# Dilated attention: two streams that keep their tiles and load the next unit over the spent one, in place of three that take new tiles for every unit

## Chip, core and metric

The kernel runs on one core of one Trainium2 chip. The metric is the device time of one execution in microseconds (us). The kernel before takes 1280.46 us (median of 3 runs, 1278.20 to 1281.73).

## What is computed

One decoder layer on x (1024 tokens, width 1024) in float32. Cut to what matters here:

```
h = RMSNorm(x) * (1 + scale(c)) + shift(c);  proj = h @ w_in   # q, k, v, z of A and of B, gates gA, gB
y_a = rms_norm(gated_delta_rule(conv_silu(q_a, k_a, v_a), g, beta)) * silu(z_a) @ w_proj_a
for gi, (win, dil) in enumerate(((128, 1), (512, 4), (2048, 16))):      # 4 heads of 64 each
    o_g, lse_g = dilated_window_attention(q_b, k_b, v_b, win, dil)      # banded blocks of 128
o_b = concat(o_g) * softmax(lse over the three groups)
y_b = (o_b * silu(z_b)) @ w_proj_b
x = x + gate(c) * ((sigmoid(gA) * y_a + sigmoid(gB) * y_b) @ w_out);  out = rms_norm(x) * final_norm_w
```

## The kernel before

Every part of the layer is a generator ("stream"). A planner in the program (`Sched`, line 136) steps the streams one by one while the kernel is built: it keeps a clock per engine with assumed costs, takes the stream of the best priority that is ready by these clocks, and so fixes, once, the order in which instructions stand on each engine. On the chip each engine works through its own list in that order and waits only on semaphores. All large products are split into a rounded high part and a rest, three float32r matmuls each. On the chip all instructions carry line 129, where the recording helper calls the engine, so rows are told apart by tile names.

Names that matter:
- `big`: 34 tiles of 128x1024 in SBUF; `mid`: 6 of 128x512; `wr`: 2, raw weights; `wh`: 6, split weights. `pj` (2 tiles of 128x1024) and `sb` (4 of 128x512) lie in PSUM. `Slots.many(2)` (line 81) takes two tiles at once, `put` gives one back.
- Attention works in 24 units (group g, head pair ti, block pair i2), listed in `todo_a` (line 1649): g = 0 (tile names ..bd 0 and 1), then 1, then 2. `attn_unit` (line 1564) takes two `big` tiles: `buf` for queries, keys and values, `sm2` for the scores. It loads q, k and v from DRAM (`qbd`, `kbd`, `vbd`), computes scores on TensorE (PE) into two `sb` tiles (`sb<-big 64*128`), masks and takes the minimum on VectorE (DVE, `CUSTOM_DVE`), takes Exp on ScalarE (ACT), transposes on PE (`sb<-cst,big`), copies back on ACT, multiplies with the values on PE (`sb<-big,big 128*64`; "PV" below), copies on DVE and stores the result to `ogd`. `buf` is given back after PV, `sm2` after the store is issued. `attn_work` (line 1643) runs this in a loop; `WORKERS` (line 39) such streams run at once, each at its own priority.
- Beside the attention PE works on the last projection products (`pair`, line 710, with `pair_out`, which for the last, z8, takes Silu on ACT in four pieces `mid<-mid` and stores them to `zd`) and, from the last third of the stage, on `tail_products` (line 1884): products pa0 to pa7 with `YA` (loaded from `yad` through `mid`, split on ACT and DVE by `ya_split`, line 1739), then pb0 to pb7 with `YB`, then the output product.
- After the last unit `attn_group` stores the statistics (`std`), `combine` (line 1668) forms the softmax over the groups (`fga`, a transpose `sb<-cst,fga` on PE, `fgd`), and two `yb_split` streams (line 1763) take j = 0 to 5 in turn: per j an `ogd` and a `zd` load, two halves of factors (`mid<-fgd`) multiplied in on DVE, one product with z (permuted for g = 1, 2), and the split into high part (ACT) and rest (DVE). pb0 uses YB[0] to YB[5] in that order, six matmuls each.
- `ya_split` takes tiles only while more than `big.debt + 1` are free, plus `RESERVE` (4) until the attention has ended.
- All DMAs concerned are issued by SyncE (SP) in one list.

Of the kernel before, what the change touches and what calls it, by code (L numbers as in the profile page):

```python
# [15 lines left out]
P = 128  # L16
# [19 lines left out]
BLOCKS = ("B11", "T2", "T1", "B21", "T3", "B22", "T4")  # L36
BLK = "x3"
BLK1 = "T1 T3 T3 T5"
WORKERS = 3
RESERVE = 4  # L40
HPRIO = 8
NW = 8
# [243 lines left out]
def hybrid_block_kernel(ctx: ExitStack, tc: tile.TileContext, x, c, norm_w, ada_w, ada_b, w_tiles, w_vb0, w_vb1,  # L286
                        w_vb2, conv_w, a_log, dt_bias, dn_norm_w, w_pa, w_pb, w_out, final_norm_w, consts, out):
    nc = tc.nc
    S = Sched(nc)
    pe, act, dve, pool, sp = S.pe, S.act, S.dve, S.pool, S.sp  # L290
# [12 lines left out]
    big = Slots(S, bigp, "big", NBIG, [P, T])  # L303
# [40 lines left out]
    vb_d = [dp.tile([T, 256], F32, name=f"vbd{g}") for g in range(3)]  # L344
# [4 lines left out]
    qb_d = [dp.tile([P, T], F32, name=f"qbd{i}") for i in range(6)]  # L349
    kb_d = [dp.tile([P, T], F32, name=f"kbd{i}") for i in range(6)]  # L350
    og_d = [dp.tile([P, T], F32, name=f"ogd{i}") for i in range(6)]
# [446 lines left out]
    ev_hb = {b: [Event() for _ in range(4)] for b in BLOCKS}  # L798
# [96 lines left out]
    ev_qb = [Event() for _ in range(6)]  # L895
    ev_kb = [Event() for _ in range(6)]
# [190 lines left out]
    ev_vbd = [Event() for _ in range(3)]  # L1087
# [473 lines left out]
    ev_og = [Event() for _ in range(3)]  # L1561
    pend = [0, 0, 0]

    def attn_unit(g, i2, ti):

        i0 = 2 * i2
        kf = max(i0 - 1, 0) if g == 0 else i0
        n_ = i0 + 2 - kf
        buf, sm2 = yield from big.many(2)
        qt, kt = buf[:, 0:256], buf[:, 256:256 + n_ * P]  # L1570
        v3 = buf[:, 640:640 + n_ * P].rearrange("p (a f) -> p a f", f=P)
        sp.dma_start(qt, qb_d[2 * g + ti][:, i0 * P:(i0 + 2) * P])
        sp.dma_start(kt, kb_d[2 * g + ti][:, kf * P:(i0 + 2) * P])
        if g == 0:
            src = vb_d[g].rearrange("(i p) f -> p i f", p=P)[:, kf:kf + n_]
        elif g == 1:
            src = vb_d[g].rearrange("(b p r) f -> r p b f", b=2, r=4)[i2]
        else:
            src = vb_d[g].rearrange("(p r) f -> p r f", r=8)[:, i0:i0 + 2]
        sp.dma_start(v3, src[:, :, ti * P:(ti + 1) * P])  # L1580
        yield
        tiles = []
        for i in (i0, i0 + 1):
            prev = (g == 0 and i > 0) or (g == 1 and i % 2 == 1)
            tiles.append((i, i % 2, (i - 1 if prev else i) - kf, 256 if prev else 128))
        sms = [sm2[:, sl] for sl in HALVES]
        pbs = yield from sb.many(2)
        for i, a, k0, nk in tiles:
            for hd in range(2):
                r = slice(64 * hd, 64 * hd + 64)  # L1590
                pe.matmul(pbs[hd][:, a * 256:a * 256 + nk], qt[r, a * P:(a + 1) * P], kt[r, k0 * P:k0 * P + nk], start=True,
                          stop=True)
        yield
        for hd in range(2):
            h4 = 2 * ti + hd
            sm = sms[hd]
            for i, a, k0, nk in tiles:
                msk = amask2 if g == 2 else amask if nk == 256 else amask[:, P:2 * P]
                dve.tensor_tensor_reduce(sm[:, a * 256:a * 256 + nk], pbs[hd][:, a * 256:a * 256 + nk], msk, -0.125, 3e38,
                                         op0=OP.add, op1=OP.min, accum_out=st_a[g][:, i, h4, 0:1])  # L1600
            sb.put()
            yield
            for i, a, k0, nk in tiles:
                s_ = sm[:, a * 256:a * 256 + nk]
                act.activation(s_, s_, AF.Exp, bias=st_a[g][:, i, h4, 0:1], scale=-1.0,
                               accum_out=st_a[g][:, i, h4, 1:2])
        yield
        pts = []
        for hd in range(2):
            pb = yield from sb.get()  # L1610
            n = 0
            for i, a, k0, nk in tiles:
                for b in range(nk // P):
                    pe.transpose(pb[:, n * P:(n + 1) * P], sms[hd][:, a * 256 + b * P:a * 256 + (b + 1) * P], ident)
                    n += 1
            yield
            pt = sms[hd]
            act.activation(pt[:, 0:n * P], pb[:, 0:n * P], AF.Copy)
            sb.put()
            pts.append(pt)  # L1620
        yield
        pb = yield from sb.get()
        n = 0
        for i, a, k0, nk in tiles:
            nb = nk // P
            for b in range(nb):
                for hd in range(2):
                    vv = v3[:, k0 + b, hd * 64:hd * 64 + 64]
                    pe.matmul(pb[64 * hd:64 * hd + 64, a * P:(a + 1) * P], vv, pts[hd][:, n * P:(n + 1) * P],
                              start=b == 0, stop=b == nb - 1)  # L1630
                n += 1
        yield
        big.put()
        dve.tensor_copy(pts[0][:, 0:2 * P], pb[:, 0:2 * P])
        sb.put()
        yield
        sp.dma_start(og_d[2 * g + ti][:, 2 * i2 * P:2 * (i2 + 1) * P], pts[0][:, 0:2 * P])
        big.put()
        pend[g] += 1
        if pend[g] == 8:  # L1640
            S.set(ev_og[g])

    def attn_work():
        while todo_a:
            g, ti, i = todo_a.pop(0)
            yield [ev_vbd[g], ev_qb[2 * g + ti], ev_kb[2 * g + ti], *ev_hb["T4"]]
            yield from attn_unit(g, i, ti)

    todo_a = [(g, ti, i) for g in range(3) for ti in range(2) for i in range(4)]

# [352 lines left out]
    for g in range(3):  # L2003
        S.add(combine(g), 7.5, f"combine{g}")
    for q in range(WORKERS):
        S.add(attn_work(), 6 + 0.1 * q, f"attnw{q}")
# [74 lines left out]
```

## Time and profile before

| | |
|---|---|
| median of 3 runs | 1280.46 us |
| the profiled execution | 1279.4 us, its span 1277.7 us |
| PE matmul busy | 1252.2 us of the span, 98% |
| DVE, ACT busy | 766.9 us, 497.9 us |
| granted PE clock, mean | 0.995 of 2.4 GHz |
| attention units on PE | from 867.6 to 1045.9 us |

The profile is one execution. A row of the timeline gives start, duration, engine, operation, output tile <- input tiles, shape, the number of merged instructions, and in brackets how long the engine sat idle before and what ended that. Matmuls are pipelined, so a merged group's duration holds the tail of its last one; start to start is the better price. "DMA to landing" counts from the issue to the arrival of the data.

### The profile page before, as it was taken

To read this page: it belongs to the slowest core of one execution; us is meant where nothing else is said; L and a number is where in the kernel's file an instruction comes from. 1 tells how busy PE (TensorE), PEld (TensorE's weight loads), DVE (VectorE), ACT (ScalarE), POOL (GpSimd) and SP (SyncE) were. 2 spreads that over 40 slices of the span, in tenths; PEclk is the share of its full clock that TensorE was granted. 3 is DMA by queue.
4 is the path that set the end of the run, shared out by engine and by line. 5 is a ranking of instruction groups with operands and counts; after the bars stand their busy time and mean duration, and the time that the engine had idled before them with its cause. 6 is when DMAs were issued, how large, how long until landed. Compare 5 with 4: busy or idle time off the path is not lost.

```text
span 1277.7 us, 19213 instructions
## 1 busy us (share of the span) xinstructions
PE 1252.2 (98%) x7302; PEld 1030.8 (81%) x7302; DVE 766.9 (60%) x1528; ACT 497.9 (39%) x1079; POOL 173.9 (14%) x128
## 2 busy tenths in 40 slices
PE   7999999999999999999999999999999999999997
PEld 3689888988888978888888888887777678878886
DVE  5845893457874367864579834555555546655533
ACT  5525622346223345233462335325555852122211
POOL 4700300033001022000320002300000000002400
PEclk9999999999999999999999999999999999999999
DMA  9534433143322262341343222645455758843422
GB/s 356 200 109 148 120 92 88 67 155 114 112 75 75 73 209 65 102 115 69 107 127 103 83 76 78 225 149 156 145 137 149 251 178 255 231 162 113 143 94 83
DMA packets 112558, 172.03 MB, mean 135 GB/s; under 512 B 41009, under 2 KB 72913, under 8 KB 112466
## 3 DMA queue, kind: packets, MB, share of 16 engines
q1 hardware_dynamic: 112322, 170.55, 42.4%
q8 instruction: 57, 0.93, 0.3%
q14 instruction: 35, 0.29, 0.1%
q10 hardware_dynamic: 144, 0.26, 0.1%
HBM read 123.40 MB, written 47.37 MB: 134 GB/s over the span
## 4 chain that ended last, share of the span: by engine, by line
PE 88%; DVE 3%; DMA 3%; ACT 2%; issue 2%; POOL 1%; SPq 0%; POOLq 0%; ACTq 0%; DVEq 0%
PE pj L129 67%; PE sb L129 22%; DVE big L129 2%; ACT big L129 1%; DMA wr<-in_w_out_dram 1%; DMA big<-kbd 1%; POOL big L129 1%; DMA big<-gd 0%; ACT wh L129 0%; DVE mid L129 0%; DVE wh L129 0%; DMA wr<-in_w_pa_dram 0%; POOL wh L129 0%; ACT L129 0%; SPq L129 0%
## 5 line engine op out<-in xcount | busy, mean ns | idle before, releaser
L129 PE MATMUL pj<-big,wh 128*128 128x512 f32 x3356 | 825.2, 398 | 0.8 <-DVE big L129 0.5
L129 PEld LDWEIGHTS pj<-big,wh 128*128 128x128 f32 x3356 | 617.2, 189 | 131.9 <-issue 9.9
L129 ACT ACTIVATE wh<-wr 128x1024 fp32r<-128x1024 f32 (+3 forms) x99 | 97.5, 985 | 239.7 <-PE pj L129 223.1
L129 DVE TENSOR_TENSOR wh<-wr,wh 128x1024 fp32r<-128x1024 f32 (+3 forms) x96 | 115.2, 1200 | 64.2 <-ACT wh L129 64.0
L129 ACT ACTIVATE big<-big 128x1024 f32<-128x1024 f32 (+2 forms) x77 | 74.1, 969 | 187.2 <-DVE big L129 133.3
L129 PE MATMUL pj<-wh,big 128*128 128x256 f32 (+2 forms) x702 | 110.6, 308 | 0.5 <-POOL wh L129 0.3
L129 PE MATMUL sb<-big,wh 128*128 128x512 f32 x368 | 105.1, 423 | 0.0
L129 PEld LDWEIGHTS pj<-wh,big 128*128 128x128 f32 x702 | 96.2, 189 | 6.2 <-POOL wh L129 0.7
L129 DVE SCALAR_TENSOR_TENSOR big<-pj,cw,big 128x1023 f32<-128x1023 f32 (+2 forms) x72 | 92.1, 1279 | 1.7
L129 PEld LDWEIGHTS sb<-big,wh 128*128 128x128 f32 x368 | 66.9, 190 | 21.1 <-issue 8.4
L129 DVE TENSOR_TENSOR big<-big,big 128x1024 f32<-128x1024 f32 (+4 forms) x44 | 57.8, 1316 | 25.9 <-ACT big L129 18.8
L129 PE MATMUL sb<-sq,big 128*128 128x128 f32 x464 | 67.9, 278 | 3.0 <-ACT sq L129 2.2
L129 PEld LDWEIGHTS sb<-sq,big 128*128 128x128 f32 x464 | 63.4, 193 | 8.8 <-ACT sq L129 3.1
L129 POOL TENSOR_TENSOR wh<-wr,wh 128x1024 fp32r<-128x1024 f32 x3 | 9.1, 3036 | 348.8 <-ACT wh L129 348.8
L129 ACT ACTIVATE big<-sb 128x512 f32<-128x512 f32 (+2 forms) x80 | 40.9, 522 | 39.6 <-PE sb L129 39.5
L129 DVE SCALAR_TENSOR_TENSOR sq<-sq,gsm,sb 128x128 f32<-128x128 f32 x48 | 16.6, 345 | 63.4 <-PE sb L129 62.2
L129 DVE CUSTOM_DVE_ANT_0 big<-sb,cst 128x128 f32<-128x128 f32 (+1 forms) x96 | 29.0, 348 | 39.7 <-PE sb L129 39.7
L129 PEld LDWEIGHTS sb<-cst,big 128*128 128x128 f32 x268 | 33.9, 145 | 22.7 <-DVE rstd L129 6.8
L129 PE MATMUL sb<-cst,big 128*128 128x128 f32 x268 | 43.5, 284 | 8.0 <-DVE rstd L129 4.9
L129 PE MATMUL pj<-big,big 128*128 128x512 f32 x210 | 49.2, 390 | 0.0
L129 ACT ACTIVATE mid<-sb 128x512 f32<-128x512 f32 (+3 forms) x48 | 24.0, 500 | 60.9 <-PE sb L129 60.5
L129 DVE TENSOR_TENSOR mid<-big 64x31 f32<-64x31 f32 (+15 forms) x124 | 41.2, 332 | 8.4 <-POOL big L129 4.9
(140 smaller groups left out, 1283.5 us busy)
## 6 DMA issues: line engine op xcount, KB each, us to landing
wr<-in_w_tiles_dram SPq DMA_DIRECT2D x64, 512.0 KB, 4.2
big<-in_ada_w_dram SPq DMA_DIRECT2D x24, 512.0 KB, 9.0
big<-in_x_dram SPq DMA_DIRECT2D x16, 512.0 KB, 5.2
gd<-big SPq DMA_DIRECT2D x16, 512.0 KB, 2.9
big<-gd SPq DMA_DIRECT2D x16, 512.0 KB, 5.2
big<-grow SPq DMA_DIRECT2D x8, 512.0 KB, 5.7
vtd<-big SPq DMA_DIRECT2D x8, 512.0 KB, 2.6
big<-vtd SPq DMA_DIRECT2D x32, 128.0 KB, 4.5
```

The source lines that it names most:

```text
L129: r = f(*a, **k)
```

## The change

A stream now takes its two tiles once. While a unit is under way it already takes the next one from `todo_a`: behind the first head's masking on DVE, with the scores computed, it issues the next unit's k and q loads over the spent ones in the same `buf`, and behind PV the next v load. The scores of a unit wait for its own k and q event, PV for its own v event. The output copy goes to another place, since `buf` and `sm2` stay in use. k is loaded ahead of q. There are two such streams, not three, so four `big` tiles are held in place of six.

```diff
-WORKERS = 3
+WORKERS = 2
-    def attn_unit(g, i2, ti):
...
-        buf, sm2 = yield from big.many(2)
-        qt, kt = buf[:, 0:256], buf[:, 256:256 + n_ * P]
-        v3 = buf[:, 640:640 + n_ * P].rearrange("p (a f) -> p a f", f=P)
-        sp.dma_start(qt, qb_d[2 * g + ti][:, i0 * P:(i0 + 2) * P])
-        sp.dma_start(kt, kb_d[2 * g + ti][:, kf * P:(i0 + 2) * P])
...
+    def attn_needs(u):
+        g, ti, i2 = u
+        return [ev_vbd[g], ev_qb[2 * g + ti], ev_kb[2 * g + ti], *ev_hb["T4"]]
+    def attn_ahead(u, buf, what, ev):
+        last, done = S.cur.last, dict(S.cur.done)
+        attn_load(u, buf, what)
+        S.set(ev)
+        S.cur.last, S.cur.done = last, done
+    def attn_unit(u, buf, sm2, evs):
...
+        yield evs[:1]
         pbs = yield from sb.many(2)
...
+            if hd == 0 and todo_a and all(e.t is not None for e in attn_needs(todo_a[0])):
+                nxt = todo_a.pop(0)
+                ahead = [Event(), Event()]
+                attn_ahead(nxt, buf, "k", ahead[0])
...
         yield
+        yield evs[1:]
         pb = yield from sb.get()
...
-        big.put()
-        dve.tensor_copy(pts[0][:, 0:2 * P], pb[:, 0:2 * P])
+        o_ = pts[0][:, 0:2 * P]
+        if nxt is None:
+            big.put()
+        else:
+            attn_ahead(nxt, buf, "v", ahead[1])
+            o_ = pts[1][:, 0:2 * P] if g == 0 else buf[:, 512:768]
+        dve.tensor_copy(o_, pb[:, 0:2 * P])
...
+        return (nxt, ahead) if nxt else (None, None)
     def attn_work():
         while todo_a:
...
+            buf, sm2 = yield from big.many(2)
...
+            while u is not None:
+                u, evs = yield from attn_unit(u, buf, sm2, evs)
```

The planner then orders everything behind the first unit anew. Three places:

On SP, in the last third of the attention (`kbd_185`, `qbd_179`, `vbd_119` are keys, queries and values of group 2's second head pair, `yad` loads feed `ya_split`, `gd` loads are gates). Before:

```order
L129 DMA big_9047<-gd_129 128x1024
L129 DMA ogd_190<-big_8856 128x256
L129 DMA big_9057<-qbd_179 128x256
L129 DMA big_9057<-kbd_185 128x256
L129 DMA big_9057<-vbd_119 128x2x128
L129 DMA mid_9073<-yad_125 128x512
```

With the change:

```order
L129 DMA big_8997<-gd_129 128x1024
L129 DMA big_7588<-kbd_185 128x256
L129 DMA big_7588<-qbd_179 128x256
L129 DMA big_8659<-vbd_119 128x2x128
L129 DMA ogd_190<-big_8659 128x256
L129 DMA mid_9036<-yad_125 128x512
```

Keys and queries of one stream's next unit now stand apart from values, and the values that stand next are the other stream's.

On ACT, where the Silu pieces of z8 (`mid<-mid`) meet the Exp of the attention (`big,sta<-big,sta`); copies of transposes are `big<-sb`, high parts of YA `big<-mid`, weight splits `wh<-wr`. Before:

```order
L129 ACT_TABLE_LOAD
L129 ACTIVATE mid_8899<-mid_8899 128x512
L129 ACTIVATE big_8766<-sb_8875 128x256
L129 ACTIVATE wh_8891<-wr_8805 128x1024
L129 ACTIVATE mid_8869<-mid_8869 128x512
L129 ACTIVATE wh_8959<-wr_8908 128x1024
L129 ACTIVATE mid_8782<-mid_8782 128x512
L129 ACT_TABLE_LOAD
L129 ACTIVATE big_8856,sta_105<-big_8856,sta_105 128x128 x2
```

With the change, from behind the third Silu piece on:

```order
L129 ACT_TABLE_LOAD
L129 ACTIVATE big_8660,sta_105<-big_8660,sta_105 128x128 x2
L129 ACTIVATE big_7589<-sb_8909 128x256
L129 ACTIVATE big_8839<-mid_8841 128x512
L129 ACTIVATE big_8839<-mid_8876 128x512
L129 ACTIVATE wh_8932<-wr_8905 128x1024
L129 ACT_TABLE_LOAD
L129 ACTIVATE mid_8772<-mid_8772 128x512
L129 ACTIVATE big_8660<-sb_8949 128x256
L129 ACTIVATE big_8660<-sb_8955 128x256
L129 ACT_TABLE_LOAD
L129 ACTIVATE big_7589,sta_105<-big_7589,sta_105 128x128 x2
```

An Exp now stands between the third and the fourth Silu piece, so this stretch has two table loads more.

On DVE, from the output of pa7 (the first row of each; `pj_9742` before, `pj_9693` now) to that of pb0 (the last). `big<-mid,big` is half a product with the factors, `128x8x128` the permuted product with z, the row of 128x768 a weight split. Before:

```order
L129 SCALAR_TENSOR_TENSOR big_9740<-big_9740,pj_9742 128x1024
L129 TENSOR_TENSOR big_9769<-mid_9781,big_9769 128x512
L129 TENSOR_TENSOR wh_9822<-wr_9686,wh_9821 128x768
L129 TENSOR_TENSOR big_9769<-mid_9828,big_9769 128x512
L129 TENSOR_TENSOR big_9778<-big_9778,big_9769 128x8x128
L129 TENSOR_TENSOR big_9865<-big_9778,big_9864 128x1024
L129 SCALAR_TENSOR_TENSOR big_9818<-big_9818,pj_9820 128x1024
```

With the change:

```order
L129 SCALAR_TENSOR_TENSOR big_9691<-big_9691,pj_9693 128x1024
L129 TENSOR_TENSOR wh_9776<-wr_9642,wh_9775 128x768
L129 TENSOR_TENSOR big_9735<-mid_9739,big_9735 128x512
L129 TENSOR_TENSOR big_9703<-mid_9757,big_9703 128x512
L129 TENSOR_TENSOR big_9706<-big_9706,big_9703 128x8x128
L129 TENSOR_TENSOR big_9735<-mid_9791,big_9735 128x512
L129 TENSOR_TENSOR big_9736<-big_9736,big_9735 128x8x128
L129 TENSOR_TENSOR big_9813<-big_9706,big_9812 128x1024
L129 TENSOR_TENSOR big_9819<-big_9736,big_9818 128x1024
L129 SCALAR_TENSOR_TENSOR big_9772<-big_9772,pj_9774 128x1024
```

Before, only YB[5] (`big_9865`) was finished between the two outputs and YB[4] ahead of them. Now the second half of YB[4] (`big_9813`) and YB[5] (`big_9819`) both stand there.

## Rows read from the trace of the kernel before

**Rows 1.** The page's busy times (us, share of the span, instructions).

```profile
PE 1252.2 (98%) x7302; PEld 1030.8 (81%) x7302; DVE 766.9 (60%) x1528; ACT 497.9 (39%) x1079; POOL 173.9 (14%) x128
```

**Rows 2.** The view of waits of PE over the whole span: who ended the idle time, us in total, times, the longest.

```profile
PE sb L129 <- DMA big<-kbd: 2.5, 4, 1.8
...
PE sb L129 <- ACT big L129: 1.3, 2, 1.0
```

**Rows 3.** The timeline of PE from 1012 to 1042 us.

```profile
1016.17 0.71 PE L129 MATMUL sb<-cst,big 128*128 128x128 f32 x2 [1.04 <-ACT big L129]
...
1018.22 0.66 PE L129 MATMUL sb<-big,big 128*64 128x128 f32 x8
1018.81 0.44 PE L129 MATMUL sb<-cst,big 128*128 128x128 f32 x2
1019.00 0.71 PE L129 MATMUL pj<-big,wh 128*128 128x512 f32 x2
...
1021.05 0.71 PE L129 MATMUL sb<-big 64*128 64x128 f32 x8 [0.20 <-DMA big<-kbd]
1021.70 0.66 PE L129 MATMUL sb<-big,big 128*64 128x128 f32 x8
1022.29 3.06 PE L129 MATMUL pj<-big,wh 128*128 128x512 f32 x12
...
1028.73 1.13 PE L129 MATMUL sb<-big 64*128 64x128 f32 x8 [1.76 <-DMA big<-kbd]
1029.79 4.17 PE L129 MATMUL pj<-big,wh 128*128 128x512 f32 x12
```

**Rows 4.** Stretches of 2 us: busy time of PE, weight loads, DVE, ACT and POOL, each with its number of instructions, then the granted clock, the DMA share and GB/s.

```profile
1028.00:1030.00 2.00, 1.27 (x9) 1.08 (x10) 0.17 (x1) 0.33 (x1) 0.00 (x0) 0.72 0.70 227
1030.00:1032.00 2.00, 2.00 (x5) 1.60 (x6) 1.97 (x10) 1.95 (x8) 0.00 (x0) 0.50 0.95 277
1032.00:1034.00 2.00, 2.00 (x10) 1.34 (x9) 0.00 (x0) 1.60 (x6) 0.00 (x0) 0.93 0.92 299
```

**Rows 5.** Stretches of 2 us at 452 us, the same columns.

```profile
452.00:454.00 2.00, 1.63 (x7) 1.35 (x6) 0.90 (x4) 0.68 (x3) 0.00 (x0) 0.50 1.09 380
454.00:456.00 2.00, 2.00 (x10) 1.76 (x9) 0.87 (x5) 0.59 (x3) 1.29 (x1) 0.64 0.99 293
```

**Rows 6.** The timeline of PE at 451 us.

```profile
451.39 0.49 PE L129 MATMUL sb<-sq,big 128*128 128x128 f32 x2 [1.80 <-ACT sq L129]
```

**Rows 7.** The chain of waits from 1018 to 1030 us: start, us, what.

```profile
1021.69 6.90 DMA big<-kbd
```

**Rows 8.** The DMA issues by form: KB each, median us from issue to landing.

```profile
mid<-fgd SPq DMA_DIRECT2D x24, 128.0 KB, 6.5
...
big<-kbd SPq DMA_DIRECT2D x18, 128.0 KB, 3.1
```

**Rows 9.** The view of waits of all engines from 865 to 1050 us, columns as in the waits of PE.

```profile
ACT big L129 <- DMA mid<-yad: 4.2, 4, 3.4
```

**Rows 10.** The timeline of ACT from 975 to 1002 us.

```profile
976.23 1.06 ACT L129 ACTIVATE wh<-Xb 128x1024 fp32r<-128x1024 f32 x1
...
992.42 0.63 ACT L129 ACTIVATE mid<-mid 128x512 f32<-128x512 f32 x1
993.07 1.28 ACT L129 ACT_TABLE_LOAD   x1
994.36 0.40 ACT L129 ACTIVATE big<-big,sta 128x128 f32<-128x128 f32 x1
...
995.52 0.58 ACT L129 ACTIVATE mid<-sb 128x512 f32<-128x512 f32 x1
...
1000.75 1.14 ACT L129 ACTIVATE big<-mid 128x512 fp32r<-128x512 f32 x2
1001.79 0.36 ACT L129 ACTIVATE big<-sb 128x256 f32<-128x256 f32 x1
```

**Rows 11.** The timeline of DVE from 1100 to 1126 us.

```profile
1109.56 2.17 DVE L129 TENSOR_TENSOR big<-big,big 128x1024 f32<-128x1024 f32 x1
1112.91 1.23 DVE L129 TENSOR_TENSOR big<-big,big 128x1024 fp32r<-128x1024 f32 x1 [1.18 <-ACT big L129]
1115.97 1.22 DVE L129 SCALAR_TENSOR_TENSOR big<-big,pj 128x1024 f32<-128x1024 f32 x1 [1.84 <-DMA big<-gd]
1117.11 0.69 DVE L129 TENSOR_TENSOR big<-mid,big 128x512 f32<-128x512 f32 x1
1117.71 0.95 DVE L129 TENSOR_TENSOR wh<-wr,wh 128x768 fp32r<-128x768 f32 x1
1118.70 0.69 DVE L129 TENSOR_TENSOR big<-mid,big 128x512 f32<-128x512 f32 x1
1119.43 2.18 DVE L129 TENSOR_TENSOR big<-big,big 128x1024 f32<-128x1024 f32 x1
1122.73 1.23 DVE L129 TENSOR_TENSOR big<-big,big 128x1024 fp32r<-128x1024 f32 x1 [1.13 <-ACT big L129]
```

**Rows 12.** The timeline of ACT from 1108 to 1126 us.

```profile
1121.64 1.06 ACT L129 ACTIVATE big<-big 128x1024 fp32r<-128x1024 f32 x1 [5.27 <-DVE big L129]
```

**Rows 13.** The timeline of PE from 1068 to 1126 us.

```profile
1070.33 53.16 PE L129 MATMUL pj<-big,wh 128*128 128x512 f32 x232
1124.02 2.34 PE L129 MATMUL pj<-big,wh 128*128 128x512 f32 x9 [0.53 <-DVE big L129]
```

More of the change, by code (lines that the diff above doesn't have):

```diff
@@ L1562, in hybrid_block_kernel, with attn_place @@
     pend = [0, 0, 0]
-    def attn_unit(g, i2, ti):
+    def attn_place(u, buf):
+        g, ti, i2 = u
         i0 = 2 * i2
@@ L1568, in attn_unit, with attn_load @@
         n_ = i0 + 2 - kf
-        buf, sm2 = yield from big.many(2)
-        qt, kt = buf[:, 0:256], buf[:, 256:256 + n_ * P]
-        v3 = buf[:, 640:640 + n_ * P].rearrange("p (a f) -> p a f", f=P)
-        sp.dma_start(qt, qb_d[2 * g + ti][:, i0 * P:(i0 + 2) * P])
-        sp.dma_start(kt, kb_d[2 * g + ti][:, kf * P:(i0 + 2) * P])
[L1574 to L1581, printed above, removed]
+        v = 640 if g == 0 else 768
+        return (buf[:, 0:256], buf[:, 256:256 + n_ * P],
+                buf[:, v:v + n_ * P].rearrange("p (a f) -> p a f", f=P), i0, kf, n_)
+    def attn_load(u, buf, what):
+        g, ti, i2 = u
+        qt, kt, v3, i0, kf, n_ = attn_place(u, buf)
+        if "k" in what:
+            sp.dma_start(kt, kb_d[2 * g + ti][:, kf * P:(i0 + 2) * P])
+            sp.dma_start(qt, qb_d[2 * g + ti][:, i0 * P:(i0 + 2) * P])
+        if "v" in what:
+            if g == 0:
+                src = vb_d[g].rearrange("(i p) f -> p i f", p=P)[:, kf:kf + n_]
+            elif g == 1:
+                src = vb_d[g].rearrange("(b p r) f -> r p b f", b=2, r=4)[i2]
+            else:
+                src = vb_d[g].rearrange("(p r) f -> p r f", r=8)[:, i0:i0 + 2]
+            sp.dma_start(v3, src[:, :, ti * P:(ti + 1) * P])
+    def attn_needs(u):
+        g, ti, i2 = u
+        return [ev_vbd[g], ev_qb[2 * g + ti], ev_kb[2 * g + ti], *ev_hb["T4"]]
[5 more added lines that the diff above has]
+    def attn_unit(u, buf, sm2, evs):
+        g, ti, i2 = u
+        qt, kt, v3, i0, kf, n_ = attn_place(u, buf)
         tiles = []
@@ L1593, in attn_unit @@
         yield
+        nxt = None
         for hd in range(2):
@@ L1632, in attn_unit @@
         yield
-        big.put()
-        dve.tensor_copy(pts[0][:, 0:2 * P], pb[:, 0:2 * P])
+        o_ = pts[0][:, 0:2 * P]
+        if nxt is None:
+            big.put()
+        else:
+            attn_ahead(nxt, buf, "v", ahead[1])
+            o_ = pts[1][:, 0:2 * P] if g == 0 else buf[:, 512:768]
+        dve.tensor_copy(o_, pb[:, 0:2 * P])
         sb.put()
         yield
-        sp.dma_start(og_d[2 * g + ti][:, 2 * i2 * P:2 * (i2 + 1) * P], pts[0][:, 0:2 * P])
-        big.put()
+        sp.dma_start(og_d[2 * g + ti][:, 2 * i2 * P:2 * (i2 + 1) * P], o_)
+        if nxt is None:
+            big.put()
         pend[g] += 1
@@ L1641, in attn_unit @@
             S.set(ev_og[g])
+        return (nxt, ahead) if nxt else (None, None)
     def attn_work():
         while todo_a:
-            g, ti, i = todo_a.pop(0)
-            yield [ev_vbd[g], ev_qb[2 * g + ti], ev_kb[2 * g + ti], *ev_hb["T4"]]
-            yield from attn_unit(g, i, ti)
+            u = todo_a.pop(0)
+            yield attn_needs(u)
+            buf, sm2 = yield from big.many(2)
+            evs = [Event(), Event()]
+            attn_load(u, buf, "k")
+            S.set(evs[0])
+            attn_load(u, buf, "v")
+            S.set(evs[1])
+            while u is not None:
+                u, evs = yield from attn_unit(u, buf, sm2, evs)
     todo_a = [(g, ti, i) for g in range(3) for ti in range(2) for i in range(4)]
```

## The prediction

> **What bounds the kernel now.** I read the page's busy times first: matmuls cover 1252.2 us of the span of 1277.7 us [rows 1]. So an edit is worth what it takes from or adds to PE's idle time, or to the time in which PE runs at its lower clock; what ACT, DVE or the DMAs gain elsewhere is worth nothing. Next the waits of PE: the attention's scores wait four times for keys, 2.5 us in all, the longest 1.8 us, and its transposes and PV twice for ACT, 1.3 us [rows 2]. That is 3.8 us, and the timeline shows where nearly all of it lies: between 1014 and 1029 us, the last third of the attention [rows 3]. The reader should see there that the scores at 1028.73 us waited 1.76 us for keys, and that the twelve matmuls behind them took 4.17 us where the same twelve at 1022.29 us took 3.06. The granted clock explains it: 0.72, 0.50 and 0.93 in three stretches of 2 us [rows 4], so PE stood at its 1.2 GHz level for most of it, and 0.56 + 1.00 + 0.14 = 1.7 us were lost. The same happened behind a wait of 1.80 us at 451 us [rows 6], with 0.50 and 0.64, again 1.7 us [rows 5]. The wait of 1.04 us [rows 3] cost no clock. The attention thus costs at most 3.8 + 1.7 = 5.5 us that a change of its loads could give back, 0.43%.
>
> **Keys and queries ahead.** The keys behind the long wait took 6.90 us from issue to arrival [rows 7]; the median is 3.1 us [rows 8]. Now a unit's keys and queries are issued right behind the previous scores of the same stream. Between a score block of the last third and the next one of its stream PE has, by the new order, some 22 matmuls of 512 columns (0.229 us each, 53.16/232, [rows 13]), three pairs of transposes, two PVs and one block of scores. Start to start these are 0.19, 0.59 and 0.65 us [rows 3]: 5.0 + 0.6 + 1.2 + 0.7 = 7.5 us, above even the 6.90. So I take the waits for keys, 2.5 us, as gone, and the fall of the clock behind them, 1.7 us. What is late next is ACT.
>
> **Two more table loads on ACT.** Before, three Silu pieces of z8 share one load; now an Exp stands between the third and the fourth, and the stretch has four loads in place of two. A load takes 1.28 us, and the Exp starts 0.01 us behind it [rows 10]. In the new order, from the copy of z8's T1 product to the second Exp pair of the unit two further on, ACT has that copy (0.58), 8 Exps (3.2), 4 loads (5.1), 3 Silus (1.9), 2 weight splits (2.1), 4 copies (1.4) and 6 halves of YA (3.4): 17.8 us, durations from [rows 10]. In the same piece of order PE has 52 matmuls (11.9), five pairs of transposes (1.0), two PVs (1.2) and two score blocks (1.3): 15.3 us. Both work through their lists in order and PE needs those Exps, so it stands for 2.5 us, in pieces of at most about 1.2 us; without the two loads the lists would be even. The halves of YA also hang on their loads, which now stand behind a weight load that waits for a split. ACT waited for them 4.2 us before, at most 3.4 at once [rows 9]; the new lateness lies between 0 and 3.4 us, and I take 0.8, nearer to the shorter ones, since half a unit's work lies ready on PE there. Together 3.3 us of new idle time.
>
> ScalarE: Activation LUTs in the Trainium skill, section What ACT_TABLE_LOAD costs, puts a switch at 1283 ns for the load and 1380 ns more for a drain, 2.66 us, which speaks against this change more strongly. The trace agrees on the load and shows no drain [rows 10]. By the page two more switches would cost 5.3 us on ACT, an estimate, and the time would come to 1285.9 us; by the rows it stays with 2.56 us on ACT.
>
> The attention as a whole: 3.3 - 5.5 = **-2.2 us**. Its bounds: -5.5 if every wait goes; if YA is late by the full 3.4 us and the clock falls once, 2.5 + 3.4 + 1.7 - 5.5 = +2.1.
>
> **The end of the attention's chain: YB.** pb0 is the first product that needs YB, 32 matmuls in for the rest of YB[5]. Before, that is the one wait behind the attention: PE ran 232 matmuls from 1070.33 to 1123.49 us and then stood 0.53 us until DVE had finished YB[5] at 1123.96 [rows 11, 13]. Counted back, pb0 began at 1116.0 and DVE began on pa7's output at 1115.97, at the same moment. From there DVE needed 8.0 us: output, factor half, weight split, factor half, permuted product, a pause of 1.1 us for ACT's high part [rows 12], rest.
>
> In the new order DVE has from pa7's output to the rest of YB[5]: output (1.14 start to start), weight split (0.97), two factor halves (0.6 and 0.73), permuted product (2.17), factor half (0.73), permuted product (2.18), and two rests (1.2 each) [rows 11]. That is 10.9 us, and 9.7 us to the rest of YB[4]; the pause for ACT is filled by the first of the two rests. DVE cannot start on any of it before pa7 has ended, since the output stands first in its list. pb0 needs the rest of YB[4] after 26 matmuls, 5.95 us, so PE stands 1.2 us for YB[4]'s high part and then about 2.4 us for its rest. Matmul 32 runs at about 11.1 us behind pa7's end, where it ran at 8.05 before: **+3.1 us**. A wait of 2.4 us is longer than both after which the clock fell [rows 3, 6], so I add the 1.7 us that each of those cost: **+4.8 us**. Bounds: 0.5 us less than 3.1 if DVE's starts pack closer, and 4.8. Behind pb0 PE is the bound up to the end, so nothing gives this back.
>
> **At nothing.** The 72 loads of the attention and its 24 stores are the same in number and size; queries and keys change places. Values are issued behind PV and needed at the next PV, one whole unit later; as before, SP stands for PV's end there, and behind it in its list wait the other stream's store and the YA loads, whose lateness is counted above. The statistics' store slips behind a weight load, but the transposes of the factors move back on PE by 16, 6 and 6 matmuls too, and YB is needed only at pb0. Two `big` tiles more are free; PE waits for no tile now. The factors of YB[5] take 6.5 us to land [rows 8] and are issued more than 9 us ahead, under pa7.
>
> **Sum.** -2.2 + 4.8 = +2.6 us. The profiled execution took 1279.4 us, so such a one would take 1282.0. It lies 1.1 us below the median of 1280.46, which I take as the base: **1283.1 us**. About 0.3%, 3.8 us, is what a measurement of this kernel can tell from no change; the forecast lies inside it.
>
> **Rivals.**
> - *The waits for keys go and the tail is hidden* (faster): -4.2 us from the keys alone, 1276.3 us. For it: the loads do move ahead by more than their landing time. Against it: DVE's list at pb0 is fixed by the order, with PE idle there already [rows 13]. 0.10.
> - *Level*: the attention loses all its 5.5 us and the wait at pb0 brings no fall of the clock: -2.4 us; with half of the attention's gain, +0.4. About 1279.5 us. 0.16.
> - *ACT becomes the bound of the last third* (slower): the two streams leave PE less other attention work while ACT switches tables, one wait grows past 1.8 us and the clock falls there too: 2.1 + 4.8 = +6.9 us, 1287.4 us. It decides from 1.8 us in one piece on. For it: 17.8 us on ACT against 15.3 on PE. Against: the waits come in pieces with matmuls between. 0.20.
> - *The loads don't come earlier*, because SP stands at a value load for PV or for a store: the 2.5 + 1.7 us stay, and the 2.5 of ACT are added to the 1.3 there was: about +1.7 in the attention and 4.8 at the tail, 1287.0 us. 0.06.
>
> **Chances.** The forecast's own case 0.48, from +0.5 to +5 us; something over a quarter of it lies beyond 3.8 us. Slower by over 0.3%: 0.13 + 0.20 + 0.06 = 0.39. Faster by over 0.3%: 0.09, most of the first rival. Within: 0.52. The range reaches from the first rival's time to the two slow ones: 1276.5 to 1287.5 us; the forecast's own is 1281.0 to 1285.5.
>
> **What would show it.** Right: the row of waits for `big<-kbd` is empty or under 0.5 us; PE waits for DVE `big` in pb0 some 3.6 us in two pieces, with a granted clock near 0.5 in a stretch behind; PE waits for ACT 2 to 4 us between the z8 product and the end of the attention, with four table loads there. Wrong: if pb0 starts without a wait, the tail's step fails and the time falls to 1276 to 1279 us; if keys are still waited for, the first step fails; if PE waits for ACT no more than before, the table loads were hidden.

## Result and profile after

| | before | after |
|---|---|---|
| median | 1278.46 us (22 runs, 1276.41 to 1283.93 and one of 7092.59) | 1284.83 us (22 runs, 1281.02 to 1289.79) |
| ratio after to before | | 1.0043, 95% interval 1.0032 to 1.0053 |
| profiled execution, span | 1279.4, 1277.7 us | 1281.23, 1279.5 us |
| granted clock, mean | 0.995 | 0.996 |

Slower by 0.43%, 5.5 us; the ratio is taken without the one slow run of the kernel before, and the two medians alone stand 6.4 us apart. The two profiled executions differ by 1.8 us only: that of before lies 0.9 us above its median, that of after 3.6 us below. So the page of after was a lucky one, and the medians have to be explained from more than one trace (first experiment). The waits of PE after, from 860 to 1130 us, which answer to [rows 2]:

```profile
PE pj L129 <- DVE big L129: 2.3, 1, 2.3
PE pj L129 <- ACT big L129: 1.8, 2, 1.4
PE sb L129 <- DMA big<-qbd: 0.4, 1, 0.4
```

The waits for keys are gone; 0.4 us for queries is left, at the first unit of all. PE's wait for ACT in the attention is one of 0.35 us, for a high part of YA, though ACT now loads its table four times there. In these timelines of PE and of ACT the wait ends 1.5 us behind the last of the four:

```profile
1020.48 1.03 PE L129 MATMUL pj<-big,wh 128*128 128x512 f32 x2 [0.35 <-ACT big L129]
```

```profile
1007.12 1.28 ACT L129 ACT_TABLE_LOAD   x1
...
1010.79 1.28 ACT L129 ACT_TABLE_LOAD   x1
...
1015.24 1.28 ACT L129 ACT_TABLE_LOAD   x1
...
1017.73 1.28 ACT L129 ACT_TABLE_LOAD   x1
1019.03 0.40 ACT L129 ACTIVATE big<-big,sta 128x128 f32<-128x128 f32 x1
```

The tail is what the forecast said. The timeline of PE, which answers to [rows 13]: two waits in pb0, 3.7 us, where there was one of 0.53.

```profile
1104.75 13.31 PE L129 MATMUL pj<-big,wh 128*128 128x512 f32 x58
1119.48 0.73 PE L129 MATMUL pj<-big,wh 128*128 128x512 f32 x2 [1.42 <-ACT big L129]
1122.52 27.74 PE L129 MATMUL pj<-big,wh 128*128 128x512 f32 x114 [2.31 <-DVE big L129]
```

The clock behind them, in stretches of 2 us (columns as in [rows 4]): it stands at its 1.2 GHz level for most of 1123 to 1127 us, which costs 0.88 + 0.82 = 1.7 us.

```profile
1123.00:1125.00 2.00, 2.00 (x7) 1.55 (x6) 0.68 (x1) 0.00 (x0) 0.00 (x0) 0.56 0.00 0
1125.00:1127.00 2.00, 2.00 (x7) 1.53 (x6) 0.39 (x1) 0.84 (x1) 0.00 (x0) 0.59 0.00 0
1127.00:1129.00 2.00, 2.00 (x10) 1.66 (x9) 1.97 (x2) 0.00 (x0) 0.00 (x0) 1.00 0.00 0
```

DVE, as in [rows 11]: nothing from 1108.2 until pa7 ends at 1112.66, and then the nine instructions, up to 1123.7 us.

```profile
1107.55 0.69 DVE L129 TENSOR_TENSOR big<-mid,big 128x512 f32<-128x512 f32 x1 [1.16 <-DMA mid<-fgd]
1112.66 1.22 DVE L129 SCALAR_TENSOR_TENSOR big<-big,pj 128x1024 f32<-128x1024 f32 x1 [4.42 <-PE pj L129]
1113.80 0.95 DVE L129 TENSOR_TENSOR wh<-wr,wh 128x768 fp32r<-128x768 f32 x1
1114.66 1.49 DVE L129 TENSOR_TENSOR big<-mid,big 128x512 f32<-128x512 f32 x2
1116.19 2.15 DVE L129 TENSOR_TENSOR big<-big,big 128x1024 f32<-128x1024 f32 x1
1118.52 0.69 DVE L129 TENSOR_TENSOR big<-mid,big 128x512 f32<-128x512 f32 x1 [0.19 <-DMA mid<-fgd]
1119.25 4.43 DVE L129 TENSOR_TENSOR big<-big,big 128x1024 f32<-128x1024 f32 x3
```

### The profile page after: what moved, and what is told of

The parts are those of the page before. It is cut to its first block, busy times and chain, and to the rows that moved or that the text cites. A ratio compares the mean times of both kernels' runs of the same rounds, so it can differ in the third digit from the quotient of the medians.

```text
span 1279.5 us, 19222 instructions
## 1 busy us (share of the span) xinstructions
PE 1252.6 (98%) x7302; PEld 1029.3 (80%) x7302; DVE 766.2 (60%) x1528; ACT 502.2 (39%) x1081; POOL 173.6 (14%) x128
## 4 chain that ended last, share of the span: by engine, by line
PE 80%; DMA 5%; DVE 5%; issue 4%; ACT 3%; POOL 2%; SPq 0%; POOLq 0%; DVEq 0%; ACTq 0%
PE pj L129 60%; PE sb L129 20%; DVE big L129 3%; DMA big<-in_x_dram 2%; ACT big L129 1%; DMA wr<-in_w_out_dram 1%; DMA big<-grow 1%; POOL big L129 1%; POOL wh L129 1%; DVE wh L129 1%; ACT L129 1%; DVE mid L129 1%; ACT wh L129 0%; DMA mid<-yad 0%; SPq L129 0%
## 5 line engine op out<-in xcount | busy, mean ns | idle before, releaser
L129 ACT ACTIVATE big<-big,sta 128x128 f32<-128x128 f32 (+1 forms) x96 | 42.2, 442 | 13.0 <-DVE sta L129 12.9
```

The lines of the kernel that those rows point to most:

```text
L129: r = f(*a, **k)
```

## The experiments

In the table each trace is cut at the first score F: front (up to F - 1 us; the same order of instructions in all these kernels, up to the attention's first loads), attention (from there to F + 182), pb0 (F + 243 to F + 275). Idle is a stretch less the time in which PE was busy; clock is the length times one minus the granted clock, both added up over pieces of 2 us. "Busy" is the time from F to the first matmul of pb0 less the idle and clock in it. Each ratio below is to the kernel before on the same chip.

| trace | front idle, clock | attention idle, clock | pb0 idle, clock | busy |
|---|---|---|---|---|
| before, page | 13.6, 3.4 | 3.83, 1.70 | 0.55, 0 | 242.6 |
| before, again | 14.6, 1.7 | 3.03, 0 | 0.85, 0 | 242.7 |
| after, page | 14.5, 1.7 | 1.19, 0 | 3.73, 1.70 | 244.7 |
| after, again | 13.9, 3.4 | 1.42, 0 | 4.60, 1.70 | 244.7 |
| after, third | 16.0, 6.9 | 2.31, 0 | 4.23, 3.40 | 245.1 |
| output moved | 16.3, 6.8 | 2.37, 0 | 2.57, 1.70 | 245.1 |
| output, split moved | 14.2, 0 | 1.18, 0 | 5.09, 3.40 | 244.2 |
| before, both moved | 16.0, 3.4 | 3.42, 1.70 | 1.70, 0 | 242.5 |
| three streams | 13.9, 3.4 | 7.13, 0 | 1.94, 0 | 244.9 |
| before, two streams | 13.6, 3.4 | 3.27, 3.42 | 16.06, 8.92 | |
| early statistics | 15.7, 5.1 | 2.32, 0 | 0.54, 0 | 245.1 |
| the same, both moved | 16.9, 6.9 | 1.29, 0 | 1.06, 0 | 244.2 |
| before, early statistics | 13.7, 3.4 | 2.91, 0 | 0.64, 0 | 242.8 |
| early statistics, Silu held | 14.1, 0 | 3.79, 0 | 2.14, 1.70 | 244.3 |

### Both kernels again

No edit.

> The kernel before, unchanged: a second profiled execution of it. Theory A: the 1.76 us wait for keys at 1028 us and the fall of the clock behind it (1.7 us) belong to the first profiled execution and not to most, so here the waits of the scores for keys are under 1.5 us in sum, the granted clock stays at 1.0 between 1014 and 1040 us and the execution takes about 1279.4 - 3 = 1276.4 us, the lowest of its 22 runs. Rival B: the same wait for keys of 1.5 to 2.0 us with the clock near 0.5 behind it, and about 1279 us.

> The changed kernel, unchanged: a second profiled execution, since the first (1281.2 us) stands 3.6 us below the median of 1284.8. Theory A: PE waits at pb0 as in the first, 1.4 us for ACT and 2.3 us for DVE, and what makes most executions longer than the first is the clock: a mean of 0.991 to 0.994 in place of 0.996, with a second fall somewhere; I expect it to be longer at pb0 (the clock at 0.5 for 6 us in place of 3.5). Rival B: the second fall lies in the attention, behind a wait of PE for ACT of over 1.5 us between 1010 and 1030 us, where four table loads stand.

> The changed kernel again, timed on the same chip as the others of this group and for a third trace: ratio to the kernel before 1.003 to 1.005; PE stands 3.5 to 4.7 us at pb0 in two pieces, the clock falls behind them (1.8 us lost), and waits for 1.2 us or less in the attention.

Before: 1276.81 us, span 1275.1. After: 1284.92 us once, and 1286.06 us (12 runs; 1.0049, 1.0033 to 1.0066). Theory A holds for the kernel before: the wait at 1028 us was 1.04 us there, and no fall of the clock followed, as the timeline and the stretches of that execution show.

```profile
1027.63 0.72 PE L129 MATMUL sb<-big 64*128 64x128 f32 x8 [1.04 <-DMA big<-kbd]
```

```profile
1026.00:1028.00 2.00, 0.96 (x13) 0.75 (x14) 0.42 (x1) 0.00 (x0) 0.00 (x0) 1.00 1.04 372
1028.00:1030.00 2.00, 2.00 (x14) 1.57 (x12) 1.66 (x10) 1.41 (x3) 0.00 (x0) 1.00 0.92 275
```

So of the 5.5 us that the forecast counted as recoverable, 1.7 belong to some executions only (two of the four traces of kernels with the old attention), and 0.8 of idle time likewise. After: the clock fell behind pb0's waits in all three traces, once for twice as long, which A had expected of the second; nothing fell in the attention, so rival B is out. What also shows is the front: 14.1 to 23.7 us are lost there over all traces, in the same order of instructions, with up to 6.9 us of it by the clock. With a spread of 9.6 us in the front alone, one page says little about 0.4%.

### What pb0 waits for: DVE's order

```diff
     def pa_out(pt, t, j):
+        if j == 7:
+            yield ev_ybs[5]
         dve.scalar_tensor_tensor(t, t, 1.0, pt, op0=OP.add, op1=OP.mult)
...
-            yield u.raw_ev
+            yield [u.raw_ev, ev_ybs[5]] if u is pb_units[2] else u.raw_ev
```

The first hunk alone is the run "output moved"; both are "output, split moved", and in the kernel before "before, both moved".

> The changed kernel with one DVE instruction moved: pa7's output product (1.14 us) stands behind the rests of YB[4] and YB[5] in DVE's list in place of ahead of them, so DVE can work on both while pa7 still runs. Theory A: the whole of PE's wait at pb0 goes, 1.4 + 2.3 us, and the fall of the clock behind it, 1.7 us: 5.4 us less than the changed kernel, 1279.4 us in the median, ratio to the kernel before 1.000 to 1.002. Rival B (most of the loss against before lies in the attention): less than 2.5 us is won, 1282.5 us or more, ratio over 1.0025.

> The changed kernel with both DVE instructions that hang on pa7's end put behind the rests of YB[4] and YB[5]: pa7's output product and the weight split of pb2 (its ACT half and its loads move with it). Moving the output alone took 1.1 us off the wait at pb0, since the weight split behind it waits for tiles that pa7 frees. Theory A: now nothing ahead of YB's work waits for pa7's end; PE's wait at pb0 falls from 3.7 to 4.6 us to under 0.8, the clock does not fall behind it, and the time is 5.5 us under that of the changed kernel on the same chip: ratio to the kernel before 0.998 to 1.000. Rival D (the loss lies elsewhere, in the 866 us of the same order): the wait goes and the ratio stays over 1.002. Rival E (YB's high parts wait for tiles of YA that pa7 frees): over 2 us of the wait stay.

> The kernel before with the same two instructions moved behind YB[5]'s rest. There PE waited only 0.5 to 0.9 us at pb0: those go, ratio to the kernel before 0.9993 to 0.9997, below what the runs can tell. If instead the ratio is over 1.002, then moving the weight split and the output costs something itself (pb1's start, pb2's weights), and the run before last must be read with that.

Measured: 1287.99 us (1.0060, 1.0041 to 1.0078), 1285.50 us (1.0040, 1.0025 to 1.0055), and for the kernel before 1281.73 us (1.0015, 1.0001 to 1.0030). Theory A failed twice. The first move took off 1.2 to 2.0 us of idle time (waits of 0.59 and 1.98 us, 2.57 in all against 3.73 to 4.60), not the whole. Why its time is nevertheless above that of the changed kernel stays open: its trace lost 23.1 us in the front, but three of its other runs took 1287.02 to 1288.61 us with a clock of 0.995, so the clock is not the reason in those. The second left even more, 3.42 and 1.67 us. In the kernel before the waits at pb0 grew to 1.18 and 0.53 us, where they were forecast to go. With pa7 out of DVE's way, the timelines of DVE and SP show what else is late:

```profile
1107.04 0.69 DVE L129 TENSOR_TENSOR big<-mid,big 128x512 f32<-128x512 f32 x1 [0.26 <-DMA mid<-fgd]
1115.31 0.69 DVE L129 TENSOR_TENSOR big<-mid,big 128x512 f32<-128x512 f32 x1 [7.58 <-DMA mid<-fgd]
1116.29 0.69 DVE L129 TENSOR_TENSOR big<-mid,big 128x512 f32<-128x512 f32 x1 [0.29 <-DMA mid<-fgd]
```

```profile
1105.67 0.34 SPq L129 DMA_DIRECT2D wr<-in_w_pb_dram  x1
...
1107.02 2.37 SPq L129 DMA_DIRECT2D mid<-fgd  x4
...
1110.06 1.17 SPq L129 DMA_DIRECT2D mid<-fgd  x2
```

DVE waits 7.58 us for factors. Four of their loads (first half of YB[5], second of YB[4]) are issued from 1107.02 us on and arrive at 1115.3 and 1116.3. They stand in SP's list behind a weight load that goes out at 1105.67. With the same moves in the kernel before DVE waited 2.30 and 2.73 us for factors. So DVE's instructions and the factors' loads are late by about as much, and taking away one leaves the other. Rival E's number came (over 2 us stay), but it named tiles of YA; the row shows DMAs.

### Tiles kept against the number of streams

```diff
-WORKERS = 2
+WORKERS = 3
```

in the changed kernel ("three streams"), and the reverse in the kernel before ("before, two streams").

> The changed kernel with three streams in place of two, and so six tiles held: the loads ahead stay, the order behind them is the planner's anew; ACT has 25 table loads as in the kernel before, and behind pa7's output DVE has five instructions up to the last rest of YB. Theory A (the loss is in the order that two streams bring at pb0, the loads ahead themselves cost nothing and save the waits for keys): no wait for keys over 0.5 us, no wait at pb0 over 0.6 us, 1276 to 1278.5 us, ratio 0.998 to 1.000. Rival C (loading over the spent tile itself costs, since k and q stand behind masks and v behind PV on SP): it stays above the kernel before, 1281 us or more.

> The kernel before with two streams in place of three, without loads ahead: the half of the change that gives tiles back, alone. Theory A (the loads ahead are what takes the waits of the scores away): PE waits for keys, queries or values at more of the units than the four of before, 3 us or more in all, and the execution takes 1283 us or more. Rival: PE has other products to do between, the waits stay under 2 us, and fewer streams alone would have done.

Three streams: 1285.69 us (1.0044, 1.0023 to 1.0065), so theory A failed here too: pb0 still waits 1.42 us for ACT and 0.52 for DVE (the clock holds), and the attention stands 7.1 us, 2.4 us for queries and 4.2 for ACT. It stays above 1281 us, as rival C said; the waits for queries, three, the longest 1.4 us, fit its reason, but the larger part is ACT's. Two streams without loads ahead: 1310.44 us in its one execution, far beyond what was expected, and not by waits in the attention: those stayed at 3.3 us, since PE took the other products meanwhile, and none of them was for keys, queries or values: fewer streams alone took the waits for keys away in that execution. But the attention ended some 45 us later, as the store of the statistics and PE's waits from 1100 to 1165 us show; the products were used up, and PE stood for YB:

```profile
1091.34 0.53 SPq L129 DMA_DIRECT2D std<-sta  x1
```

```profile
PE pj L129 <- ACT big L129: 16.6, 3, 6.5
PE pj L129 <- DVE big L129: 4.7, 3, 1.7
```

That puts the rest of the matter in view: YB hangs on a chain from the statistics on, and the pa products are its cover.

### The start of that chain

```diff
     def attn_group(g):
-        yield ev_og[g]
+        yield ev_sx[g]
...
                                accum_out=st_a[g][:, i, h4, 1:2])
+        pens[g] += 1
+        if pens[g] == 8:
+            S.set(ev_sx[g])
         yield
...
-            yield [ev_fg[g], ev_zd[8 + j]]
+            yield [ev_fg[g], ev_og[g], ev_zd[8 + j]]
```

> The changed kernel with one thing moved: a group's statistics are stored right behind its last Exp, in place of behind its last output store. In the changed kernel the last store of statistics stood on SP behind a weight load and went out at 1049.7 us, 11 us behind the last Exp; it starts the chain statistics, softmax factors, YB. Theory F (the attention's end came 3.3 us earlier on PE, but this store, which hangs on a weight load, did not, and so the chain lost its lead over pa7's end): the store goes out near 1040 us, behind pa7's output DVE has six instructions again in place of nine, PE's wait at pb0 falls from 3.7 to 4.6 us to 0.6 or less with no fall of the clock: 5 to 6 us less than the changed kernel, ratio to the kernel before 0.998 to 1.001. Rival G (the loads for YB[4] and YB[5] wait for tiles that pa7 frees, and the statistics don't matter): over 2 us of the wait stay, ratio over 1.003.

> As the run before, and pa7's output and pb2's weight split also stand behind YB[5]'s rest on DVE (which alone, without the early statistics, left the wait at 5 us, since the factors landed late). Theory F: now DVE and the loads both have lead; no wait at pb0 (under 0.3 us), ratio to the kernel before 0.997 to 1.000. Rival G: as in the run before, over 2 us stay.

> The kernel before with the early statistics alone. Its wait at pb0 was 0.5 to 0.9 us and is set by the six DVE instructions behind pa7's output, which stay six: ratio to the kernel before 0.999 to 1.001. Against it the changed kernel with the early statistics shows what the attention alone brings: by theory F 1.5 to 3 us less for the tiles that are kept (waits of 3.0 to 3.8 us in the attention against 0.8 to 1.0); if it is not faster than this one, the loads ahead bring nothing that can be measured.

Measured: 1280.26 us, ratio to before 0.9987 (0.9969 to 1.0005), where the changed kernel had 1.0043 and 1.0049. The interval meets neither of those two (1.0032 to 1.0053, 1.0033 to 1.0066): it gives back the whole loss, with the order that the planner makes behind it. With both DVE moves on top 1280.42 us (0.9998, 0.9983 to 1.0012), which adds nothing; 1.06 us of wait stay at pb0, where under 0.3 was forecast, as DVE waits 2.67 and 2.31 us for factors there. The kernel before with it: 1281.53 us (1.0006, 0.9990 to 1.0022). Theory F, number by number: in the kernel before the last Exp ends at 1040.6 and in the changed kernel at 1039.0. The store stood behind a weight load before too, and in the changed kernel stands behind one more, as the timelines of SP show, first before, then after:

```profile
1048.08 0.33 SPq L129 DMA_DIRECT2D wr<-in_w_pa_dram  x1
1048.51 0.38 SPq L129 DMA_DIRECT2D big<-gd  x1
1048.94 0.52 SPq L129 DMA_DIRECT2D std<-sta  x1
```

```profile
1044.43 0.33 SPq L129 DMA_DIRECT2D wr<-in_w_pa_dram  x1
...
1049.34 0.33 SPq L129 DMA_DIRECT2D wr<-in_w_pa_dram  x1
1049.73 0.53 SPq L129 DMA_DIRECT2D std<-sta  x1
```

With the early store, SP, PE and DVE:

```profile
1046.27 1.42 SPq L129 DMA_DIRECT2D std<-sta  x1
...
1090.77 0.43 SPq L129 DMA_DIRECT2D big<-ogd  x1
```

```profile
1126.92 13.26 PE L129 MATMUL pj<-big,wh 128*128 128x512 f32 x57 [0.53 <-DVE big L129]
```

```profile
1118.88 1.22 DVE L129 SCALAR_TENSOR_TENSOR big<-big,pj 128x1024 f32<-128x1024 f32 x1 [2.45 <-PE pj L129]
1120.02 0.95 DVE L129 TENSOR_TENSOR wh<-wr,wh 128x768 fp32r<-128x768 f32 x1
1120.89 1.40 DVE L129 TENSOR_TENSOR big<-mid,big 128x512 f32<-128x512 f32 x2
1122.33 2.18 DVE L129 TENSOR_TENSOR big<-big,big 128x1024 f32<-128x1024 f32 x1
1125.64 1.23 DVE L129 TENSOR_TENSOR big<-big,big 128x1024 fp32r<-128x1024 f32 x1 [1.13 <-ACT big L129]
```

The store goes out 1.0 us behind the last Exp, which ended at 1045.3 in this execution (its front took 4.9 us longer than on the page of after). From the store to pb0's first matmul there are 66.8 us in both traces of the kernel before, 62.7 in all three of the changed kernel and 72.4 here (1046.27 to 1118.68). Of the 4.1 us that the change took, 2.4 are the store's, which went out 10.7 us behind the last Exp in place of 8.3; the other 1.7 are pb0's, which came 73.4 us behind that Exp in place of 75.2. YB[4]'s loads went out 19.2 us ahead of pa7's end in the kernel before; in the changed kernel, on the page of after, from 1099.49 us on, 13.2 us ahead; here from 1090.77, 28.1 us ahead, so YB[4] is done by then and DVE has only YB[5] left. Its six instructions from pa7's output to YB[5]'s rest wait for no load, only for ACT's high part (1.13 us), and the same 0.53 us remain as before the change.

The gain in the attention is seen in the traces but not resolved in the time: 0.9987 against 1.0006 for the kernel before with the same store, with intervals that overlap.

### The table loads of ACT

```diff
+        came, ev_all = [0], Event()
         def sink(r, q, src):
             if func is not None:
+                came[0] += 1
+                if came[0] == 4:
+                    S.set(ev_all)
+                elif came[0] > 1:
+                    yield ev_all
```

on top of the early statistics.

> The changed kernel with the early statistics, and the second and third Silu piece of z8 held back until the fourth, so that ACT has 25 table loads in place of 27 (2 times 1.28 us). The forecast put 2.5 us of new waits of PE on the two loads. Theory F (they are hidden: with 27 loads PE waited only 0.35 us for ACT behind them): PE's idle time in the attention stays between 0.7 and 1.6 us, where it was 1.2 to 2.3, and the ratio to the kernel before lies within 0.0015 of the 0.9987 of the run with the early statistics alone. Rival H (the loads cost what was forecast): PE's waits for ACT vanish and the ratio is 0.997 or less.

Measured: 1285.20 us, ratio 1.0036 (1.0020 to 1.0051). Neither theory had that. With 25 loads PE waited more for ACT in the attention, not less:

```profile
1020.64 0.43 PE L129 MATMUL sb<-big,big 128*64 128x128 f32 x2 [0.98 <-ACT big L129]
1021.68 0.65 PE L129 MATMUL sb<-big,big 128*64 128x128 f32 x6 [0.60 <-ACT big L129]
...
1029.81 0.43 PE L129 MATMUL sb<-big,big 128*64 128x128 f32 x2 [0.93 <-ACT big L129]
1030.85 0.65 PE L129 MATMUL sb<-big,big 128*64 128x128 f32 x6 [0.61 <-ACT big L129]
```

and at pb0 2.1 us again, with a fall of the clock: the new order put pa7's output behind a factor half that stood 8.24 us for its load. So the store of the statistics alone doesn't decide it either: it went out 77.2 us ahead of pb0 here, and 76.6 in the kernel with three streams, where pb0 waited too and DVE stood 8.78 us for a factor load. In both, four factor loads went out in a row behind a weight load (from 1107.59 and from 1112.49 us). For the two loads the run is no clean test, since the planner moved more than them; it only shows that as few as 25 don't bring fewer waits. That they are hidden in the changed kernel rests on its own trace, 0.35 us.

## Why the prediction was right or wrong

Forecast 1283.1 us, measured 1284.83; +2.6 us against +5.5. The direction and both places were right, the size was about half.

- *Waits for keys gone*: right, in every trace of the changed kernel. That it takes the loads ahead for this is not shown: two streams without them had none either, at a price elsewhere.
- *Fall of the clock behind them, -1.7*: a mis-sized term. It was in the one execution that I read; in the second the wait was 1.04 us and nothing fell. As base I took the median, but the gain from one execution that was longer than its median.
- *ACT, +3.3 us of new idle time*: wrong in size. Four loads came as forecast, and PE waited 0.35 and 0.36 us for ACT in two traces, and 1.2 us for ACT and DVE in the third. My sum set 17.8 us of ACT against 15.3 of PE as if both entered the piece level and PE needed each Exp at once; no run tells which of the two was wrong. The rival of an attention bound by ACT fell with it. The table loads themselves are as priced: the Exp starts at 1019.03, 0.02 us behind the load of 1.28 us; the drain that the Trainium skill (ScalarE: Activation LUTs, What ACT_TABLE_LOAD costs) adds to each switch shows in this trace no more than in the one before.
- *The attention, -2.2*: idle and clock together came to 1.2, 1.4 and 2.3 us against 5.5 and 3.0, in the mean -2.6. Against that stands a term that I did not have, +1.5 us of busy time (last section). -1.1 in all.
- *Tail, +4.8*: two waits of 1.2 and 2.4 us were forecast; 1.42 and 2.31 were on the page, with the fall behind them, and DVE took 11.0 us where 10.9 was forecast. That the page met the two waits so closely is luck in part: the second and third traces had 2.35 + 2.24 and 2.54 + 1.70 us, and 3.4 us of clock in one. Mean 6.5 us against 0.7 before: +5.8.
- *At nothing*: two costs there were not nothing. I saw the statistics' store slip behind a weight load and wrote it off, since YB is needed only at pb0. But the chain from that store had no lead to spare, as the wait of 0.53 us before shows, and lost 4.1 us of it: 2.4 by the store's slip, 1.7 since pb0 came that much nearer to the last Exp. And the factors' loads were not early enough: without DVE's part they alone hold pb0. DVE's nine instructions, from which I worked out the time, were how the loss showed; with the store moved they are six again. How much of that is the store and how much the rest of the order that the planner then made, no run separates.

By these traces the sum is -1.1 + 5.8 = +4.7 us, within the measured 4.1 to 6.8. What is left, about 1 us, can't be placed: the front varies by more. The level rival and the faster one needed a pb0 without a fall or without a wait; neither occurred.

## What to carry to other kernels

A gain on the busy engine only counts as far as every chain that must meet it later moves too: write down, for each store or load that starts such a chain, what it stands behind in its queue, and how much lead it had. Of a wait in one profiled execution, ask whether the next one has it, above all where a fall of the clock hangs on it. If a wait has two causes of like length, taking one away shows nothing; look for what is ahead of both.

## What the runs showed of the hardware that was not expected

Whether the clock falls behind a wait is not settled by the wait's length. The wait of 1.80 us at 451 us is in every trace, and the clock fell behind it in nine of fourteen. In the attention of the old kernels it fell behind 1.76 and 1.20 us, and not behind 1.04 and 1.06; with three streams PE waited 1.75 us at once and nothing fell. What a fall cost came in steps: 1.7 or 3.4 us.

PE's busy time from the first score to pb0 was 242.5 to 242.8 us in four traces of the old attention and 244.2 to 245.1 in the nine with loads ahead. Three product matmuls, 0.7 us, account for a part: they stand ahead of the first score in the old order and behind it in the new one. About 1.5 us are left, for the same work. The groups by form from 866 to 1112 us, before (second execution) and after (second execution), seem to show where: the transposes and the scores cover 23.4 + 12.8 + 10.6 = 46.8 us before and 24.0 + 13.2 + 11.1 = 48.3 after, at the same counts. But what a group covers includes tails that overlap with the next group. Priced start to start in the same two traces, the transposes take 14.0 us in both, the scores 20.1 and 20.7, the products in `pj` 132.5 and 135.2 (0.7 of it the three more), those in `sb` 57.0 and 56.1, PV 19.1 and 18.8. So it lies in the products more than in the small matmuls; the products in `pj` now stand in 56 groups in place of 48, and whether that is the reason is not shown.

```profile
L129 PE MATMUL sb<-cst,big 128*128 128x128 f32 x140 | 23.4, 277 | 1.1 <-ACT big L129 1.1
...
L129 PE MATMUL sb<-big 64*128 64x256 f32 x88 | 12.8, 391 | 0.0
L129 PE MATMUL sb<-big 64*128 64x128 f32 x104 | 10.6, 306 | 1.6 <-DMA big<-kbd 1.6
```

```profile
L129 PE MATMUL sb<-cst,big 128*128 128x128 f32 x140 | 24.0, 278 | 0.3
...
L129 PE MATMUL sb<-big 64*128 64x256 f32 x88 | 13.2, 392 | 0.0
L129 PE MATMUL sb<-big 64*128 64x128 f32 x104 | 11.1, 307 | 0.7 <-DMA big<-qbd 0.6
```
